# The recurrence stage of a one-core encoder step: two-operand work moved from GpSimd to VectorE, small products in the chunk banks, the elementwise stage cut in two

## The chip, the core and the metric

The kernel runs on one core of a Trainium2 chip. The metric is the device time of one execution in microseconds (us), less is better. A core has a matrix engine (TensorE, PE in the rows; PEld is its weight load), VectorE (DVE), ScalarE (ACT), GpSimd (POOL) and SyncE (SP). Each engine takes its instructions in the order in which they stand in its own queue, and waits on semaphores for the others. [...]

## The reference

One layer for two groups of requests at once, a prompt of 1024 tokens and 8 streams of 16 tokens: 1152 rows in all. The left branch of the layer is a recurrence over tokens:

```python
h = rms_norm(x, norm1_g)
p = h @ w_in                     # one projection: recurrence | attention | gates
u = pr + (shifted - pr) * mu     # token shift
r, k, v, wl, al, gl = split(u)
decay = exp(-exp(-softplus(-(w0 + tanh(wl) @ w2)) - 0.5))
a = sigmoid(a0 + al @ a2);  g = sigmoid(gl) @ g2
kk = k * k_k;  kk = kk * rsqrt(sum(kk * kk) + 1e-12)      # per head
k = k * (1 + (a - 1) * k_a)
# per token and head:
#   S = S * decay + (S @ -kk) (kk * a)^T + v k^T ;  y = S @ r
y = groupnorm(y) * lnx_g + lnx_b
o_a = (y + sum(r * k * r_k) * v) * g
o_b = forgetting_attention(...)
x = x + (sigmoid(g_a) * (o_a @ p_a) + sigmoid(g_b) * (o_b @ p_b)) @ w_out
x = x + swiglu(rms_norm(x))
```

There are 8 heads of 64, d_model is 1024, all in float32 (matrix products in two parts, high and low).

## The kernel before

The program runs through four stages. From 0 to 198 us x is normalised and turned, and the first tiles of the input projection are made. From 198 to 838 us the recurrence runs, from 838 to 1100 us the attention, and to the end the merge, the output product and the feed-forward part.

**The recurrence** goes by six units of 192 tokens (`rwkv_unit`, L527): five of the prompt, with 3 chunks of 64, and a last one whose second and third chunk's worth are the eight streams. A unit first writes the factors `BK` (L541 to L543) and `TT` (L550, L552), transposes v (L558), and makes the gram products (L587) in three rounds of four chunk-heads. Masks follow: `masked` (L572) on VectorE for the half that goes to `GB`, a copy by ScalarE (L590) and then a mask by GpSimd (the call behind L592) for the half that goes into `TT`. Then comes the inverse of a triangular factor: the copies L603, the half `goff` (L605, GpSimd), 15 steps of L616 and L618 on VectorE, transposes L630 and L632, and four groups of products of 32x32 (L651, L659 and L662, L679, L688), with the additions to `x1c` and `x3` by VectorE between (recorded at L387, the helper `hi`, which gives an instruction a high priority). Then the chunks, one after the other: the state product into `cp` (L724), the decayed state `sts` (GpSimd), `solve_u` (L707: VectorE copies `w_sb`, TensorE multiplies at L714, VectorE and ScalarE copy the two halves back), the product with the keys into `cp` (L736), the new state `st` by VectorE, and the outputs (L731, L747).

**Beside a unit** run two generators. `prologue` (L422) of the next unit makes its decays, norms and factors, with small products at L437/L438 and L446, exponentials, and the elementwise lines L484 to L491. `epilogue` (L500) of the unit before makes the group norm (L505, L511) and the gate product (L523). `step(nxt)` and `step(last)` run them on to their next `yield`; so the places of these calls in the unit set the order on TensorE.

**The projection** fills TensorE's gaps. It is a queue `fq` of 1032 pieces (43 weight tiles of 24 pieces; a piece is three products of 128x384, L151 to L153), from which `D(n)` takes n; `W(us)` (L389) takes as many as us / 0.52, rounded up. A weight tile is loaded by `load_w` (L139): a DMA, a rounded copy `hi_c` by ScalarE (L145), and the residue `lo_c` (L146), which `w_in_tile` (L211) gives to GpSimd. Pieces that are not taken by the end of the stage are taken at the attention.

**The order** on TensorE is the order of the code (a manual schedule). On the other engines a scheduler sets it before the program is built; each engine then works strictly in that order.

**PSUM** has eight banks: three of `gm` for the projection, two of `ms` for all small products, and one each of `y0`, `y1` (a unit's outputs) and `ch` (the chunk's `cp`).

In the rows, all buffers of the tag `t` are called t, whatever variable they hold.

Of the kernel before, what the change touches and what calls it, by code (L numbers as in the profile page):

```python
# [8 lines left out]
F32 = mybir.dt.float32  # L9
# [44 lines left out]
def hybrid_kernel(ctx: ExitStack, tc: tile.TileContext, d, o):  # L54
# [156 lines left out]
    def w_in_tile(c0, M):  # L211
        return load_w(wp1, d["w_in"][0, :, c0:c0 + M].rearrange("(k p) m -> p k m", p=P), NK, M, f"c{c0}", eng=GP)

# [140 lines left out]
    def ms():  # L354
        return psr.tile([P, 512], F32, tag="ms", name="ms")

    def tt_(tag="t", bufs=NSLOT):
        return rp.tile([P, W2], F32, tag=tag, name=tag, bufs=bufs)
# [15 lines left out]
    def pr4(t_):  # L374
        return t_.rearrange("p (y t) -> p y t", y=4)
# [46 lines left out]
    def prologue(u_, us, out):  # L422
# [10 lines left out]
        for z in range(2):  # L433
            pw, pa_ = ms(), ms()
            for y in (2 * z, 2 * z + 1):
                cs = slice((y % 2) * UT, (y % 2 + 1) * UT)
                T.matmul(pw[:, cs], lw[0:64, y * P:(y + 1) * P], LT[0:64, :], start=True, stop=True)  # L437
                T.matmul(pa_[:, cs], lw[64:128, y * P:(y + 1) * P], LT[64:128, :], start=True, stop=True)  # L438
            for y in (2 * z, 2 * z + 1):
                cs = slice((y % 2) * UT, (y % 2 + 1) * UT)  # L440
                S.activation(sw[:, y * UT:(y + 1) * UT], pw[:, cs], AF.Sigmoid, bias=pc("rwkv_w0", y))
                S.activation(a[:, y * UT:(y + 1) * UT], pa_[:, cs], AF.Sigmoid, bias=pc("rwkv_a0", y))
            yield
        for gs in HALF:
            ps = ms()
            T.matmul(ps[:, :2 * UT], ones_b, kk[:, gs], start=True, stop=True)  # L446
            S.activation(kk[:, gs], ps[:, :2 * UT], AF.Ln, bias=kkb)
# [27 lines left out]
        if ncp == NC3:  # L475
            V.tensor_tensor(sc[:, :, 0:ncp - 1], sc[:, :, 0:ncp - 1], dmn[:, :, 1:ncp], op=mult)
        else:
            scs = rp.tile([P, 4, NB], F32, tag="scs", name="scs", bufs=1)
            S.copy(scs.unsqueeze(3), pr4(dd)[:, :, C:UT].rearrange("p x (b t) -> p x b t", t=DT)[:, :, :, DT - 1:DT])

        k2 = tt_()
# [18 lines left out]
    def epilogue(u_, yT, bv, LG):  # L500

        sq = tt_()
        for gs in HALF:
            ps = ms()
            T.matmul(ps[:, :2 * UT], ones_b, yT[:, gs], start=True, stop=True)  # L505
            V.scalar_tensor_tensor(yT[:, gs], in0=ps[:, :2 * UT], scalar=-1.0 / C, in1=yT[:, gs], op0=mult, op1=add)
        S.activation(sq, yT, AF.Square)
        yield
        for gs in HALF:
            ps = ms()  # L510
            T.matmul(ps[:, :2 * UT], ones_b, sq[:, gs], start=True, stop=True)  # L511
            S.activation(sq[:, gs], ps[:, :2 * UT], AF.Ln, bias=gnb, scale=1.0 / C)
# [7 lines left out]
        for z, gs in enumerate(HALF):  # L520
            ps = ms()
            for y in range(2):
                T.matmul(ps[:, y * UT:(y + 1) * UT], lg[:, (2 * z + y) * P:(2 * z + y + 1) * P], LG, start=True, stop=True)  # L523
            V.tensor_tensor(yT[:, gs], yT[:, gs], ps[:, :2 * UT], op=mult)
        dma2(oa_s.rearrange("(c p) t -> p c t", p=P)[:, :, u_ * UT:(u_ + 1) * UT], pr4(yT))

    def rwkv_unit(u_, us, nu, pre, last):  # L527
# [14 lines left out]
        V.tensor_tensor(BK[:, :, 2, :], ch3(k2), ch3(e3), op=mult)  # L542
        GP.tensor_tensor(BK[HS[1], :, 0, :], ch3(k2)[HS[1]], ch3(e3)[HS[1]], op=mult)  # L543

# [6 lines left out]
        for hd in range(2):  # L551
            GP.tensor_tensor(TT[HS[hd], :, hd, 1, :], ch3(ur)[HS[hd]], ch3(e2)[HS[hd]], op=mult)  # L552
        SV = [ch3(tt_()) for _ in range(2)]
# [17 lines left out]

        def masked(dst, src, c0, hs, eng=V):  # L572
            n0 = 0
            late_ = [final and (c0 + n) % NC3 >= 1 for n in range(4)]
            while n0 < 4:
                n1 = n0 + 1
                while n1 < 4 and late_[n1] == late_[n0]:
                    n1 += 1
                mk = (gmask_s if late_[n0] else gmask)[hs].unsqueeze(1).broadcast_to([hs.stop - hs.start, n1 - n0, 2, C])
                eng.tensor_tensor(dst[:, n0:n1], src[hs, n0:n1], mk, op=mult)  # L580
                n0 = n1

        for c0 in range(0, NC12, 4):
            pg = [psr.tile([P, 4, 2, C], F32, tag="ms", name="gram") for _ in range(2)]
            for c in range(4):
                for hd in range(2):
                    T.matmul(pg[hd][:, c], both(hd, c0 + c), TT[HS[hd], c0 + c, hd], start=True, stop=True)  # L587
            for hd in range(2):
                masked(GB[HS[hd], c0:c0 + 4], pg[hd], c0, HS[hd])
                S.copy(TT[OP[hd], c0:c0 + 4, hd], pg[hd][OP[hd]])  # L590
            W(2.1)
        step(last)  # L592
        for hd in range(2):
            for c0 in range(0, NC12, 4):
                masked(TT[OP[hd], c0:c0 + 4, hd], TT[:, c0:c0 + 4, hd], c0, OP[hd], GP)
        gab, grb = GB[:, :, 0, :], GB[:, :, 1, :]
# [7 lines left out]
        goff = tt_()[:, 0:NC12 * 32].rearrange("p (c t) -> p c t", t=32)  # L604
        GP.tensor_tensor(goff, dg[:, 0:NC12, :], low16.unsqueeze(1).broadcast_to([P, NC12, 32]), op=mult)  # L605
        L = inv_tile()
# [25 lines left out]
        V.transpose(XL[:, 0:32, :], X[:, 0:32, :])  # L632
        step(nxt)
        step(last)
        W(2.6)
        step(nxt)
        W(2.1)
        step(nxt)
        W(2.1)
        step(nxt)  # L640
        step(last)
        W(4.2)
        xd = XL[:, 0:32, 0:NC12].rearrange("p t c -> p c t")
        QS = [slice(32 * q, 32 * q + 32) for q in range(4)]
        NB32 = NC12 * 32
        step(nxt)

# [6 lines left out]
        p03 = p0.rearrange("p (c t) -> p c t", t=32)  # L654
        W(1.0)
        ps, ps1 = ms(), ms()
# [45 lines left out]
        Y = [psr.tile([P, 2, NC3, C], F32, tag=f"y{z}", name=f"yps{z}", bufs=1) for z in range(2)]  # L702

# [3 lines left out]
        def solve_u(cp, c, y0, n):  # L707
# [8 lines left out]
            hi(S.copy, SV4[1][HS[1], ysl, c, :], cp[HS[1], 1, ysl])  # L716
            W(1.0)

        for c in range(ncp):
            cp = psr.tile([P, 2, 4, 64], F32, tag="ch", name="cp", bufs=1)  # L720
            for y in range(4):
# [4 lines left out]
            for hd, hs in enumerate(HS):  # L726
                hi(GP.tensor_tensor, sts[hs], SV4[hd][hs, :, c, :], sc[hs, :, c:c + 1].broadcast_to([64, 4, 64]), op=mult)
            for y in range(4):
# [31 lines left out]
        def streams(z):  # L760
# [16 lines left out]
            for cc in range(2):  # L777
                c = 1 + cc
                bsl = slice(4 * cc, 4 * cc + 4)
                bm = bds.unsqueeze(2).broadcast_to([P, 4, 64])  # L780
                cp = psr.tile([P, 2, 4, 64], F32, tag="ch", name="cps", bufs=1)
                ams = []
# [970 lines left out]
```

## Time and profile before

| | before |
|---|---|
| median of 3 runs | 2134.14 us (2127.28 to 2136.34) |
| the profiled execution | 2131.44 us |
| its span | 2129.7 us |
| TensorE busy, share of the span | 1987.0 us, 93% |
| VectorE | 1215.4 us, 57% |
| ScalarE | 835.1 us, 39% |
| GpSimd | 408.6 us, 19% |
| mean granted clock of TensorE | 0.966 |

TensorE is busy for 93% of the span. Its clock is granted between half and full speed by the chip, and a matmul in a stretch with a low clock counts as busy for longer. The table is a mean over stages with different limits; the rows below take the recurrence apart.

### The profile page before, as it was taken

The numbers are of one execution on the slowest core, as the hardware profiler recorded it, in microseconds if no ns is written. First come the engines' busy times: TensorE is split into PE (matmuls) and PEld (weight loads), VectorE is DVE, ScalarE is ACT, GpSimd is POOL, SyncE is SP. The second block draws the span as 40 slices with busy tenths as digits, with TensorE's granted clock in tenths as the row PEclk, the third lists the DMA queues.
The fourth block names the chain that finished last, engine by engine and source line by source line (L and its number), as shares of the span: only waits on it lengthen the run. The fifth ranks groups of instructions, "written<-read, shape, count | busy, mean of one in ns | idle before, by whom it ended". The sixth has DMA issues, their size and how long they took to land. (4 is left out here: it accounts for less than half of the span.)

```text
span 2129.7 us, 38310 instructions
## 1 busy us (share of the span) xinstructions
PE 1987.0 (93%) x15472; PEld 1803.2 (85%) x15472; DVE 1215.4 (57%) x2267; ACT 835.1 (39%) x1606; POOL 408.6 (19%) x445
## 2 busy tenths in 40 slices
PE   7999988889999998979989899999999999799998
PEld 7998877778787887767877799899999999788887
DVE  5112576555746645467755617966666666464445
ACT  5323444463635432456654325532332233121113
POOL 3322423233342410010015326000000000000004
PEclk9999999999999999889989999999999999899999
DMA  5332333222221223776547535232122221542212
GB/s 169 102 99 88 105 93 91 64 62 68 64 65 53 74 65 90 193 196 166 155 152 259 190 114 175 70 97 70 63 82 63 82 85 53 204 148 84 84 64 89
DMA packets 221541, 228.42 MB, mean 107 GB/s; under 512 B 41534, under 2 KB 195796, under 8 KB 221364
## 3 DMA queue, kind: packets, MB, share of 16 engines
q1 hardware_dynamic: 158916, 159.33, 25.3%
q10 hardware_dynamic: 61920, 64.54, 9.0%
q8 instruction: 122, 2.00, 0.4%
q0 software_dynamic: 528, 2.10, 0.3%
q14 instruction: 55, 0.45, 0.1%
HBM read 157.00 MB, written 68.98 MB: 106 GB/s over the span
## 5 line engine op out<-in xcount | busy, mean ns | idle before, releaser
L151 PE MATMUL gm<-hh,hi_c 128*128 128x384 f32 (+1 forms) x1032 | 376.3, 365 | 0.9 <-DVE vl L927 0.5
L153 PE MATMUL gm<-hh,lo_c 128*128 128x384 f32 (+1 forms) x1032 | 353.8, 343 | 1.6 <-POOL lo_c L146 1.6
L152 PE MATMUL gm<-hl,hi_c 128*128 128x384 f32 (+1 forms) x1032 | 354.6, 344 | 0.0
L151 PEld LDWEIGHTS gm<-hh,hi_c 128*128 128x128 f32 (+1 forms) x1032 | 198.0, 192 | 16.7 <-issue 3.1
L152 PEld LDWEIGHTS gm<-hl,hi_c 128*128 128x128 f32 (+1 forms) x1032 | 197.9, 192 | 4.7 <-issue 0.8
L153 PEld LDWEIGHTS gm<-hh,lo_c 128*128 128x128 f32 (+1 forms) x1032 | 197.5, 191 | 4.4 <-POOL lo_c L146 2.2
L1684 POOL TENSOR_TENSOR yo<-x,gF 128x512 f32<-128x512 f32 x17 | 21.9, 1289 | 760.8 <-DVE x L1668 751.1
L1664 PE MATMUL dn<-hi_d,ah 128*128 128x512 f32 x396 | 156.1, 394 | 12.4 <-ACT ah L1371 11.3
L1665 PE MATMUL dn<-lo_d,ah 128*128 128x512 f32 x396 | 155.4, 393 | 0.0
L1666 PE MATMUL dn<-hi_d,al 128*128 128x512 f32 x396 | 155.0, 393 | 0.0
L146 POOL TENSOR_TENSOR lo_c<-raw_c,hi_c 128x1024 fp32r<-128x1024 f32 (+1 forms) x43 | 103.3, 2403 | 245.6 <-ACT hi_c L145 243.2
L1668 DVE TENSOR_TENSOR x<-x,dn 128x512 f32<-128x512 f32 x108 | 73.9, 687 | 118.8 <-PE dn L1666 115.9
L1664 PEld LDWEIGHTS dn<-hi_d,ah 128*128 128x128 f32 x396 | 75.2, 190 | 29.3 <-ACT ah L1371 12.2
L265 DVE SCALAR_TENSOR_TENSOR su<-gm,omu,sh 128x384 f32<-128x384 f32 (+1 forms) x42 | 24.1, 573 | 122.5 <-ACT sh L261 95.9
L1666 PEld LDWEIGHTS dn<-hi_d,al 128*128 128x128 f32 x396 | 75.2, 190 | 16.3 <-DVE al L1372 0.5
L1665 PEld LDWEIGHTS dn<-lo_d,ah 128*128 128x128 f32 x396 | 75.3, 190 | 15.4
L1371 ACT CAST ah<-raw_act 128x1152 fp32r<-128x1152 f32 x22 | 25.6, 1162 | 159.7 <-PE dn L1665 141.4
L1469 PE MATMUL po<-hi_o,mh 128*128 128x256 f32 x288 | 82.5, 287 | 0.0
L1470 PE MATMUL po<-lo_o,mh 128*128 128x256 f32 x288 | 82.3, 286 | 0.0
L1471 PE MATMUL po<-hi_o,ml 128*128 128x256 f32 x288 | 82.1, 285 | 0.0
L145 ACT CAST hi_c<-raw_c 128x1024 fp32r<-128x1024 f32 (+1 forms) x43 | 44.3, 1031 | 74.1 <-PE gm L152 60.4
L1552 DVE TENSOR_TENSOR buf<-buf,m 128x256 f32<-128x256 f32 (+1 forms) x88 | 39.8, 453 | 45.4 <-PE m L1530 45.4
(495 smaller groups left out, 5482.2 us busy)
## 6 DMA issues: line engine op xcount, KB each, us to landing
raw_c<-in_w_in SPq DMA_DIRECT2D x42, 512.0 KB
raw_act<-a_s SPq DMA_DIRECT2D x22, 576.0 KB
raw_w_gate<-in_w_gate SPq DMA_DIRECT2D x22, 512.0 KB
raw_w_up<-in_w_up SPq DMA_DIRECT2D x22, 512.0 KB
raw_d<-in_w_down SPq DMA_DIRECT2D x22, 512.0 KB
g_s<-sg ACTq DMA_DIRECT2D x48, 192.0 KB
raw_o<-in_w_out SPq DMA_DIRECT2D x16, 512.0 KB
u_s<-su ACTq DMA_DIRECT2D x42, 192.0 KB
```

Of the source, the lines that this page charges most:

```text
L145: S.copy(hi[:, :, c0:c0 + M], raw)
L146: eng.tensor_tensor(lo[:, :, c0:c0 + M], raw, hi[:, :, c0:c0 + M].bitcast(F32), op=sub)
L151: T.matmul(ps, wh(k), xh(k), start=(k == 0), stop=False)
L152: T.matmul(ps, wh(k), xl(k), start=False, stop=False)
L153: r = T.matmul(ps, wl(k), xh(k), start=False, stop=(k == nk - 1))
L1469: T.matmul(ps[:, :Q], mh, hi, start=(k == 0), stop=False)
L1470: T.matmul(ps[:, :Q], mh, lo, start=False, stop=False)
L1471: T.matmul(ps[:, :Q], ml, hi, start=False, stop=(k == NK - 1))
L1664: T.matmul(ps, ah[:, ts_], wh[:, cs], start=(x == 0), stop=False)
L1665: T.matmul(ps, ah[:, ts_], wl[:, cs], start=False, stop=False)
L1666: T.matmul(ps, al[:, ts_], wh[:, cs], start=False, stop=(x == n - 1))
L1668: r = V.tensor_tensor(xs, xs, ps, op=add)
```

## The change

It does four things.

1. *GpSimd loses its work with two operands.* The residue `lo_c`, the third block of `BK`, the halves of `TT` with `ur * e2`, `goff` and `sts` go to VectorE. GpSimd keeps fills and copies.
2. *Masks from PSUM.* Both halves of the gram products are masked by VectorE straight from PSUM. ScalarE's copies (L590) and the masks of GpSimd are gone. The second round of grams uses the banks y0 and y1 in place of `ms`.
3. *Small products through the chunks' banks.* A new helper `xs` gives out y0, y1 and ch in turn; the products L437, L446, L505, L511 and L523 use it. The bonus product (L496) stays in `ms`.
4. *The elementwise stage in two parts.* `prologue` has one more `yield`, ahead of `k2`. What stands behind it (L484 to L491) is now run on by a `step(nxt)` behind the inverse's additions. The calls of `step` and `W` between the transposes of the inverse and its first product are placed anew, `W` behind `p0` and behind the additions takes more, and the last chunk's `W` too.

In the code after the change the lines have other numbers: L387 is L395, L437 is L445, L446 is L454, L484 is L493, L491 is L500, L505 is L514, L511 is L520, L523 is L532, L541 is L550, L550 is L559, L552 is L561, L580 is L589, L659 is L669, L714 is L726, L724 is L736 and L736 is L748.

```diff
     def w_in_tile(c0, M):
-        return load_w(..., NK, M, f"c{c0}", eng=GP)
+        return load_w(..., NK, M, f"c{c0}")
...
+    turn = [0]
+    def xs():
+        turn[0] += 1
+        tag = ("y0", "y1", "ch")[turn[0] % 3]
+        return psr.tile([P, 512], F32, tag=tag, name="xs", bufs=1)
...
-            pw, pa_ = ms(), ms()
+            pw, pa_ = xs(), xs()
...
-            ps = ms()
+            ps = xs()
             T.matmul(ps[:, :2 * UT], ones_b, kk[:, gs], start=True, stop=True)
...
+        yield
         k2 = tt_()
...
-        GP.tensor_tensor(BK[HS[1], :, 0, :], ch3(k2)[HS[1]], ch3(e3)[HS[1]], op=mult)
+        V.tensor_tensor(BK[HS[1], :, 0, :], ch3(k2)[HS[1]], ch3(e3)[HS[1]], op=mult)
...
-            GP.tensor_tensor(TT[HS[hd], :, hd, 1, :], ch3(ur)[HS[hd]], ch3(e2)[HS[hd]], op=mult)
+            V.tensor_tensor(TT[HS[hd], :, hd, 1, :], ch3(ur)[HS[hd]], ch3(e2)[HS[hd]], op=mult)
...
-            pg = [psr.tile([P, 4, 2, C], F32, tag="ms", name="gram") for _ in range(2)]
+            pg = [(psr.tile([P, 512], F32, tag=f"y{x}", name="gram", bufs=1) if c0 == 4 else ms())
+                  .rearrange("p (c y t) -> p c y t", c=4, y=2) for x in range(2)]
...
                 masked(GB[HS[hd], c0:c0 + 4], pg[hd], c0, HS[hd])
-                S.copy(TT[OP[hd], c0:c0 + 4, hd], pg[hd][OP[hd]])
+                masked(TT[OP[hd], c0:c0 + 4, hd], pg[hd], c0, OP[hd])
             W(2.1)
         step(last)
-        for hd in range(2):
-            for c0 in range(0, NC12, 4):
-                masked(TT[OP[hd], c0:c0 + 4, hd], TT[:, c0:c0 + 4, hd], c0, OP[hd], GP)
...
-        GP.tensor_tensor(goff, dg[:, 0:NC12, :], low16..., op=mult)
+        V.tensor_tensor(goff, dg[:, 0:NC12, :], low16..., op=mult)
...
         step(nxt)
+        W(1.5)
         step(last)
-        W(2.6)
+        W(1.5)
         step(nxt)
-        W(2.1)
+        W(1.5)
         step(nxt)
-        W(2.1)
+        W(1.5)
+        step(last)
+        W(1.0)
         step(nxt)
-        step(last)
-        W(4.2)
+        W(1.5)
+        step(nxt)
+        W(3.1)
...
-        step(nxt)
...
         hi(S.copy, p0, ps[:, :NB32])
-        W(1.0)
+        W(2.1)
...
                 hi(GP.memset, x3[qs, :, 0:32], 0.0)
-        W(2.1)
+        step(nxt)
+        W(2.6)
...
-            W(1.0)
+            W(1.5 if c == ncp - 1 else 1.0)
...
-                hi(GP.tensor_tensor, sts[hs], ...)
+                hi(V.tensor_tensor, sts[hs], ...)
...
         for _ in prologue(0, us, pre):
-            W(6.0)
+            W(5.0)
```

In all 636 pieces of the projection stand in the recurrence stage, 621 before; 330 stand ahead of it (332 before), and 66 are left for behind it (79 before).

Three places of the new order follow, all in the third unit that makes a next one (unit 2 by the code's count). On TensorE, ahead of the inverse's first product, stand the norm product of the next unit (line 446; `ones_b` is a constant of block sums) and the gate product of the unit before (line 523), among pieces of the projection (lines 151 to 153). Before:

```order
L153 MATMUL gm<-hh_100,lo_c_5285 128x384
L151 MATMUL gm<-hh_100,hi_c_5284 128x384
L152 MATMUL gm<-hl_103,hi_c_5284 128x384
L153 MATMUL gm<-hh_100,lo_c_5285 128x384
L446 MATMUL ms<-t,ones_b 128x384 x2
L523 MATMUL ms<-lo_3309,lg 128x192 x4
```

After, where the norm product is line 454 and the gate product line 532:

```order
L532 MATMUL xs<-lo_3312,lg 128x192 x4
L151 MATMUL gm<-hh_98,hi_c_5399 128x384
L152 MATMUL gm<-hl_101,hi_c_5399 128x384
L153 MATMUL gm<-hh_98,lo_c_5400 128x384
L151 MATMUL gm<-hh_98,hi_c_5399 128x384
L152 MATMUL gm<-hl_101,hi_c_5399 128x384
L153 MATMUL gm<-hh_98,lo_c_5400 128x384
L454 MATMUL xs<-t,ones_b 128x384 x2
```

The gate product has moved ahead of the norm product, with two pieces between, and both take a bank from `xs`.

On VectorE, from the elementwise stage of the next unit to the first chunk (`w_sb` is the copy that the chunk's second product reads; the rows of 32 partitions are the additions to `x1c` and `x3`). Before:

```order
L485 TENSOR_TENSOR u<-t,u 128x768
L487 TENSOR_TENSOR t<-t 128x768
L491 SCALAR_TENSOR_TENSOR t<-u,prm 128x192 x4
L541 SCALAR_TENSOR_TENSOR BK<-t 128x12x64
L542 TENSOR_TENSOR BK<-u,t 128x12x64
L387 TENSOR_TENSOR t<-ms,inv 32x384 x2
L387 TENSOR_TENSOR t<-ms,inv 32x12x32 x4
L387 COPY w_sb<-cp 128x256
L387 COPY t<-cp 64x4x64
```

After:

```order
L146 TENSOR_TENSOR lo_c_4820<-raw_c_4817,hi_c_4819 128x1024
L395 TENSOR_TENSOR t<-ms,inv 32x384 x2
L395 TENSOR_TENSOR t<-ms,inv 32x12x32 x4
L493 TENSOR_SCALAR t<-t,prm,oka 128x192 x4
L494 TENSOR_TENSOR u<-t,u 128x768
L496 TENSOR_TENSOR t<-t 128x768
L500 SCALAR_TENSOR_TENSOR t<-u,prm 128x192 x4
L550 SCALAR_TENSOR_TENSOR BK<-t 128x12x64
L551 TENSOR_TENSOR BK<-u,t 128x12x64
L395 COPY w_sb<-cp 128x256
L552 TENSOR_TENSOR BK<-u,t 64x12x64
L395 COPY t<-cp 64x4x64
```

The additions have moved ahead of the second part (lines 493 to 500) and of two blocks of the next unit's `BK`; `w_sb` now stands behind all of these, and a residue (line 146) ahead of the additions. In the other units with a next one the order is alike; the residue stands right ahead of the additions in four units of the six.

On VectorE, the last chunk of the same unit, with the new state `st` at its end. Before:

```order
L387 COPY w_sb<-cp 128x256
L550 TENSOR_TENSOR TT<-t 64x12x64 x2
L387 COPY t<-cp 64x4x64
L387 TENSOR_TENSOR st<-cp,sc 128x256
L387 TENSOR_TENSOR st<-st,sts 128x256
```

After:

```order
L395 COPY w_sb<-cp 128x256
L559 TENSOR_TENSOR TT<-t 64x12x64 x2
L395 COPY t<-cp 64x4x64
L146 TENSOR_TENSOR lo_c_5202<-raw_c_5199,hi_c_5201 128x1024
L561 TENSOR_TENSOR TT<-u,t 64x12x64
L395 TENSOR_TENSOR st<-cp,sc 128x256
L561 TENSOR_TENSOR TT<-u,t 64x12x64
L395 TENSOR_TENSOR st<-st,sts 128x256
```

Behind the copy of `cp` into t a residue and the first half of `ur * e2` (line 561) have come ahead of the state, and the second half stands between its two instructions.

## Rows read from the trace of the kernel before

**Rows 1.** busy time by stage: start:end, us, each engine's busy time (count), granted clock, DMA
```profile
198.00:838.00 640.00, 579.63 (x6347) 501.71 (x6346) 376.73 (x678) 293.59 (x532) 203.77 (x175) 0.95 0.25 74
838.00:861.00 23.00, 18.29 (x98) 17.38 (x96) 10.26 (x17) 2.87 (x7) 3.21 (x3) 0.85 0.62 155
```

**Rows 2.** waits of TensorE, 198 to 838 us: line, releaser, total us, times, longest
```profile
PE ms L523 <- ACT t L447: 14.0, 4, 6.8
PE cp L736 <- ACT t L387: 10.9, 5, 3.5
PE ms L511 <- ACT t L627: 7.9, 3, 4.4
PE ms L437 <- ACT t L441: 6.3, 4, 2.2
PE lfps L859 <- DVE sg L853: 4.9, 1, 4.9
PE ms L659 <- ACT t L387: 4.1, 2, 3.7
```

**Rows 3.** timeline, unit 3: start us, us, engine, line, operation, idle before
```profile
476.22 1.05 ACT L447 ACTIVATE t<-ms,kkb 128x384 f32<-128x384 f32 x2
476.85 2.93 PE L523 MATMUL ms<-lo,lg 128*128 128x192 f32 x8 [6.82 <-ACT t L447]
```

**Rows 4.** timeline, VectorE and GpSimd side by side
```profile
357.06 2.42 POOL L146 TENSOR_TENSOR lo_c<-raw_c,hi_c 128x1024 fp32r<-128x1024 f32 x1 [6.21 <-ACT hi_c L145]
357.30 2.32 DVE L616 TENSOR_TENSOR tmp<-inv 128x128 f32<-128x128 f32 x1
361.18 0.86 ACT L627 COPY t<-ms 128x384 f32<-128x384 f32 x2 [3.38 <-DVE inv L618]
```

**Rows 5.** timeline, last chunk of a unit
```profile
513.43 3.46 DVE L550 TENSOR_TENSOR TT<-t 64x768 f32<-64x768 f32 x2
513.48 5.09 POOL L552 TENSOR_TENSOR TT<-u,t 64x768 f32<-64x768 f32 x2 [0.93 <-PE yps L731]
516.92 0.42 DVE L387 COPY t<-cp 64x256 f32<-64x256 f32 x1
517.84 0.69 PE L736 MATMUL cp<-t 128*64 128x64 f32 x16 [1.86 <-ACT t L387]
```

**Rows 6.** timeline, unit 5 from the additions to the first chunk
```profile
671.26 5.16 DVE L387 TENSOR_TENSOR t<-ms,inv 32x384 f32<-32x384 f32 x6 [1.35 <-PE ms L662]
678.20 0.43 DVE L387 COPY w_sb<-cp 128x256 f32<-128x256 f32 x1 [1.77 <-PE cp L724]
679.28 0.68 PE L714 MATMUL cp<-w_sb,t 64*64 64x64 f32 x16
```

**Rows 7.** timeline, elementwise stage of unit 2
```profile
386.54 1.25 DVE L484 TENSOR_SCALAR t<-t,prm,oka 128x192 f32<-128x192 f32 x4
387.82 0.96 DVE L485 TENSOR_TENSOR u<-t,u 128x768 f32<-128x768 f32 x1
```

**Rows 8.** the instructions of line 491: ns min/median/max, first and last start
```profile
L491 DVE SCALAR_TENSOR_TENSOR t<-u,prm x24: 405/408/2537, 216.4 to 667.8; 128x192 f32<-128x192 f32 x24
```

**Rows 9.** busy time in windows of 4 us, columns as in rows 1
```profile
224.00:228.00 4.00, 1.97 (x8) 1.98 (x9) 3.99 (x7) 0.00 (x0) 0.00 (x0) 0.63 0.79 226
228.00:232.00 4.00, 4.00 (x15) 4.00 (x14) 2.29 (x7) 1.81 (x3) 0.00 (x0) 0.52 0.53 157
```

**Rows 10.** groups of GpSimd, 198 to 838 us: busy us, mean ns, idle before, releasers
```profile
L146 POOL TENSOR_TENSOR lo_c<-raw_c,hi_c 128x1024 fp32r<-128x1024 f32 x26 | 63.1, 2428 | 122.5 <-ACT hi_c L145 120.1 <-issue 1.9 <-POOL sts L387 0.3
L580 POOL TENSOR_TENSOR TT<-TT,gmask 64x512 f32<-64x512 f32 (+1 forms) x38 | 42.0, 1106 | 35.4 <-ACT TT L590 33.9
L552 POOL TENSOR_TENSOR TT<-u,t 64x768 f32<-64x768 f32 x12 | 30.1, 2508 | 11.9 <-ACT t L469 8.2 <-PE yps L731 3.3
L387 POOL TENSOR_TENSOR sts<-t,sc 64x256 f32<-64x256 f32 x32 | 22.0, 689 | 77.5 <-DVE t L387 76.5
```

**Rows 11.** groups of VectorE, whole program
```profile
L1372 DVE TENSOR_TENSOR lo_d<-raw_d,hi_d 128x1024 fp32r<-128x1024 f32 x22 | 26.8, 1221 | 10.7 <-ACT hi_d L1371 10.7
```

More of the change, by code (lines that the diff above doesn't have):

```diff
@@ L211, in w_in_tile @@
     def w_in_tile(c0, M):
-        return load_w(wp1, d["w_in"][0, :, c0:c0 + M].rearrange("(k p) m -> p k m", p=P), NK, M, f"c{c0}", eng=GP)
+        return load_w(wp1, d["w_in"][0, :, c0:c0 + M].rearrange("(k p) m -> p k m", p=P), NK, M, f"c{c0}")
     ahead = []
@@ L503, in epilogue @@
         for gs in HALF:
-            ps = ms()
+            ps = xs()
             T.matmul(ps[:, :2 * UT], ones_b, yT[:, gs], start=True, stop=True)
@@ L509, in epilogue @@
         for gs in HALF:
-            ps = ms()
+            ps = xs()
             T.matmul(ps[:, :2 * UT], ones_b, sq[:, gs], start=True, stop=True)
@@ L520, in epilogue @@
         for z, gs in enumerate(HALF):
-            ps = ms()
+            ps = xs()
             for y in range(2):
@@ L570, in rwkv_unit, with masked @@
         GB = rp.tile([P, NC12, 2, C], F32, tag="GB", name="GB", bufs=1)
-        def masked(dst, src, c0, hs, eng=V):
+        def masked(dst, src, c0, hs):
             n0 = 0
@@ L579, in masked @@
                 mk = (gmask_s if late_[n0] else gmask)[hs].unsqueeze(1).broadcast_to([hs.stop - hs.start, n1 - n0, 2, C])
-                eng.tensor_tensor(dst[:, n0:n1], src[hs, n0:n1], mk, op=mult)
+                V.tensor_tensor(dst[:, n0:n1], src[hs, n0:n1], mk, op=mult)
                 n0 = n1
         for c0 in range(0, NC12, 4):
-            pg = [psr.tile([P, 4, 2, C], F32, tag="ms", name="gram") for _ in range(2)]
+            pg = [(psr.tile([P, 512], F32, tag=f"y{x}", name="gram", bufs=1) if c0 == 4 else ms())
+                  .rearrange("p (c y t) -> p c y t", c=4, y=2) for x in range(2)]
             for c in range(4):
@@ L604, in rwkv_unit @@
         goff = tt_()[:, 0:NC12 * 32].rearrange("p (c t) -> p c t", t=32)
-        GP.tensor_tensor(goff, dg[:, 0:NC12, :], low16.unsqueeze(1).broadcast_to([P, NC12, 32]), op=mult)
+        V.tensor_tensor(goff, dg[:, 0:NC12, :], low16.unsqueeze(1).broadcast_to([P, NC12, 32]), op=mult)
         L = inv_tile()
@@ L701, in rwkv_unit @@
                 hi(V.tensor_tensor, SV4[hd][hs, :, 0, :], st[hs], dmn[hs, :, 0:1].broadcast_to([64, 4, 64]), op=mult)
-        Y = [psr.tile([P, 2, NC3, C], F32, tag=f"y{z}", name=f"yps{z}", bufs=1) for z in range(2)]
+        Y = [psr.tile([P, 512], F32, tag=f"y{z}", name=f"yps{z}", bufs=1)[:, 0:2 * UT]
+             .rearrange("p (y c t) -> p y c t", y=2, c=NC3) for z in range(2)]
         def yout(z):
@@ L716, in solve_u @@
             hi(S.copy, SV4[1][HS[1], ysl, c, :], cp[HS[1], 1, ysl])
-            W(1.0)
+            W(1.5 if c == ncp - 1 else 1.0)
         for c in range(ncp):
-            cp = psr.tile([P, 2, 4, 64], F32, tag="ch", name="cp", bufs=1)
+            cp = psr.tile([P, 512], F32, tag="ch", name="cp", bufs=1).rearrange("p (z y t) -> p z y t", z=2, y=4)
             for y in range(4):
@@ L726, in rwkv_unit @@
             for hd, hs in enumerate(HS):
-                hi(GP.tensor_tensor, sts[hs], SV4[hd][hs, :, c, :], sc[hs, :, c:c + 1].broadcast_to([64, 4, 64]), op=mult)
+                hi(V.tensor_tensor, sts[hs], SV4[hd][hs, :, c, :], sc[hs, :, c:c + 1].broadcast_to([64, 4, 64]), op=mult)
             for y in range(4):
@@ L780, in streams @@
                 bm = bds.unsqueeze(2).broadcast_to([P, 4, 64])
-                cp = psr.tile([P, 2, 4, 64], F32, tag="ch", name="cps", bufs=1)
+                cp = psr.tile([P, 512], F32, tag="ch", name="cps", bufs=1).rearrange("p (z y t) -> p z y t", z=2, y=4)
                 ams = []
```

## The prediction

> **What bounds the kernel now.** I read the busy time by stage first. In the recurrence stage, 198 to 838 us, TensorE works 579.63 us of 640, VectorE 376.73, ScalarE 293.59 and GpSimd 203.77, and the granted clock is 0.95 [rows 1]. TensorE is therefore the bound, but with two holes: the time in which it stands, about 60 us, and the clock, (1 - 0.95) x 640 = 32 us of full-speed work. No other engine is full, so what an edit is worth is what it does to the waits of TensorE.
>
> So I went next to the waits of TensorE in that stage [rows 2]. Six of them hold 48.1 us in 19 waits. Line 523 (the gate product of the epilogue) waits 14.0 us, four times; line 736 (the state product) 10.9, five times; line 511 (the variance product) 7.9; line 437 (the decay products of the prologue) 6.3; line 859 (a transpose of the projection) 4.9; line 659 (the inverse's second product) 4.1.
>
> Then I looked in the timeline at what each of them really waits for. Line 523 waits 6.82 us in unit 3 and starts as soon as ScalarE has read the first half of the norm product (line 447, at 476.22 us) [rows 3]. The gate product needs nothing of line 447. It needs a buffer of the two that `ms` has, and both hold norm products. Line 511 is of the same kind: it waits for ScalarE's copy L627, the reader of the key transposes, which is not its input either [rows 2]. Behind that there is a second cause: GpSimd's L146 runs from 357.06 to 359.48 us, and VectorE's L616, 128 short elements a partition, starts 0.24 us later and ends at 359.62, just after it; ScalarE's copy stands 3.38 us behind VectorE's chain [rows 4]. Line 736 has the same pair behind it: two instructions L550 of VectorE take 3.46 us beside two L552 of GpSimd (5.09 us), the next copy of VectorE starts only at 516.92, and TensorE stands 1.86 us [rows 5].
>
> These rows read as a lock: a VectorE instruction with two operands in SBUF does not go on while GpSimd has one in hand. The Trainium skill says the same ("SBUF — State Buffer", section "SBUF: two separate sides"): the port pair that the two engines share is given to one of them for a whole instruction and the other blocks fully. The trace agrees (2.32 us for L616); by that rule the change would get VectorE's time back, not TensorE's, and the sum below needs only the rows.
>
> **The change part by part.**
> *Two-operand work leaves GpSimd.* In the stage GpSimd has 26 L146 of 2428 ns, 48 masks (38 in the row shown), 12 L552 and 32 `sts` [rows 10], beside six L543 and six L605. On VectorE an L146 should take what the same subtraction takes later in the program, 1221 ns [rows 11]: 26 x 1.22 = 32 us more load, the rest some 30 us more, and about 40 us of lock time back. So VectorE stands near 377 + 62 - 40 = 400 of 640 us and does not become the bound by its sum. What matters is where those instructions stand in its order.
>
> *Last chunk.* L550 no longer meets L552, so two of L550 cost about 1.9 us in place of 3.46 and one more piece lies ahead of line 736. The five waits of 10.9 us [rows 2] fall to about 1.6: -9.3. Now L146 and the halves of `ur*e2` stand near the state's instructions there; that is priced below.
>
> *Products in the idle banks.* The gate product now comes ahead of the norm product and takes a bank of y0, y1 and ch. Its cause is gone: -14.0. Line 511 has a bank of its own: -7.9. Line 859 waits for VectorE's L853 once, behind a locked chain: -4.9. All three from [rows 2]. The decay products rotate over three banks where two pairs need four, so the second pair still waits for the first's reader; cover falls from 5 pieces to 3. I keep its 6.3 us (bounds 0 and 11.5). Line 659 is not touched: 4.1 stays (0 to 8.2).
>
> *The elementwise stage in two parts.* This is the step that costs. The second part is put behind the inverse's additions, and in VectorE's new order it stands ahead of the first chunk's `w_sb`, for which the first chunk's second product waits. Its length: line 484 1.25 us, four instructions of 128x768 at 0.96 (lines 485, 487, 541, 542) [rows 7], four of line 491 at 0.405, its minimum [rows 8]: 1.25 + 3.84 + 1.62 = 6.7 us. In unit 5 of before, the additions start at 671.26, `w_sb` at 678.20 and the product that reads it at 679.28, 8.0 us after the additions; VectorE is idle for 1.77 us before `w_sb` [rows 6]. After: additions about 5.1, part two 6.7, `w_sb` 0.4: ready at 12.2 us, where TensorE wants it at 8.0. The number of pieces between does not change. So TensorE gets a new wait of about 4 us, in units 0 to 4 (the last has no next unit): +20. Bounds: 2.4 us each if TensorE runs at a low clock there and comes later, 5.2 if L146 falls between: 12 to 26; below that only if the order on the chip hides it (rival B).
>
> *L146 and the halves on VectorE ahead of chain work.* In four units an L146 stands right ahead of the additions, in some ahead of the state. I take 4 x 1.2 plus a little: +6 (0 to 12).
>
> *Clock.* Each wait costs more than itself: from 224 to 228 us TensorE works 1.97 of 4 us and the granted clock is 0.63 of full speed (2.4 GHz); in the next 4 us, where it works all the time, it is 0.52, the lower level of 1.2 GHz for nearly all of it [rows 9]. 32 us over 19 waits is 1.7 us each. Thirteen waits go (4 + 3 + 1 + 5), five come: 8 x 1.7 = 14 us back (0 to 32).
>
> The Trainium skill says of this ("TensorE: Matmul & The Clock Gate", section "HAM oscillation — how this bites in real kernels") that repeated gaps of TensorE throw its clock back each time. By that rule gaps that are only moved give no clock back, the term of 14 us would be 0 and the time near 2121. That is rival C, priced below from rows.
>
> *Pieces.* Thirteen pieces of the projection move from behind the stage into it (0.52 us each, 6.8 us). They are work either way, and in the stage they fill waits that I have already counted: 0 (-7 to +7). Behind the stage the short stretch of 838 to 861 us has TensorE busy 18.29 of 23 us at a clock of 0.85 [rows 1], so little is lost or won there.
>
> **Sum.** -14.0 - 7.9 - 4.9 - 9.3 + 20 + 6 - 14 = -24. The profiled execution took 2131.4 us (span 2129.7), 2.7 below the median of 2134.1. 2131.4 - 24 = 2107, and from the median 2110. I give **2108**.
>
> **The rivals.**
> *A, slower: VectorE stands behind the residues.* L146 needs ScalarE's L145 first, and GpSimd waited for that 120.1 us in 26 times, 4.6 each [rows 10]. On GpSimd nothing is behind it. On VectorE, which works in order, everything is: the inverse's chain, the copies of the chunks. If half of the 26 stand so for half of that wait, 13 x (2.3 + 1.2) = 45 us more, 2107 + 45 = 2152. It decides from 38 us on, where 2107 passes 2145, 1.5 us for each of the 26. Against it: GpSimd's wait counts from its own last instruction, often long before, and VectorE has 240 us of room.
> *B, the second part is hidden.* If the additions end earlier (their 5.16 us in unit 5 hold a lock with an L146 [rows 6]) or more work of TensorE lies ahead, the new wait is gone with its clock: 2107 - 20 - 5 x 1.7 = 2079. Against it: the order puts all of part two ahead of `w_sb`.
> *C, the clock does not come back.* The waits that are left and the five new ones keep it at 0.95: 2107 + 14 = 2121, with the upper bound of the new wait 2127: at the edge of 0.5% and within it. For it speaks that the new waits are long (4 us).
> *D, the masks and residues were off the path and nothing of their removal shows:* only the waits of the ring and of line 859 go (-26.8), the new ones come (+20): 2131.4 - 6.8 = 2125, within 0.5% too. Against it stand rows 4 and 5, in which the lock reaches TensorE.
>
> **How the numbers follow.** Forecast (2093 to 2122) 0.42; B 0.20; C and D 0.23; A 0.15. 0.5% is about what a measurement of this kernel tells from no change, 10.7 us: below 2123.5 is faster, above 2144.8 slower. Faster: 0.40 of the forecast and 0.20 of B, 0.60. Same: 0.02, 0.23 and a fifth of A (its weak end), 0.28. Slower: 0.12. The range goes from B, 2077, to the point where A begins to count, 2140.
>
> **What would show it.** Right: no wait at the gate product and the variance product; L491's successor at a mean near 405 ns, not 1067; a new wait of TensorE for `w_sb`, about 4 us, five times; the state product's wait below 0.5 us; a stage shorter by 20 to 30 us at a clock of 0.96 or more. Wrong: a stage as long as before with TensorE waiting for VectorE's residues or copies behind an L146 (A), or no `w_sb` wait at all (B), or the same clock with fewer waits (C). The prediction falls altogether if the first part of the elementwise stage, which now runs beside other VectorE work, makes the inverse late.

## The result and the profile after

The changed kernel takes 2107.86 us, the median of 4 runs (2106.34 to 2110.43), where the kernel before took 2133.06 us, the median of four; in the jobs of the experiments below it took 2127 to 2129. The ratio is 0.9899, with a 95% interval of 0.988 to 0.9918: 1% faster. The profiled execution has a span of 2108.4 us against 2129.7. The forecast was 2108. One execution of a later kernel took 2714.26 us at a granted clock of 0.649, far from its others, and is left out of that kernel's time.

First the busy time by stage again, cut where the attention's first product starts (line 991 before, 1003 after): each engine's busy time (count), then the granted clock. Before:

```profile
198.00:839.08 641.08, 580.71 (x6354) 502.70 (x6353) 377.42 (x679) 293.62 (x532) 203.77 (x175) 0.95 0.25 74
```

After:

```profile
198.00:826.07 628.07, 584.86 (x6432) 508.99 (x6432) 422.68 (x810) 269.32 (x497) 22.95 (x47) 0.96 0.27 78
```

Two things are to be seen here. In the stage TensorE stands 641.08 - 580.71 = 60.4 us before and 628.07 - 584.86 = 43.2 us after: 17 us fewer. And it works 4.2 us longer there although it makes 25 more pieces of the projection in that window (648 products of line 151 against 623), which is 13 us of work: the other work, and the same work, therefore cost some 9 us less, and the granted clock is 0.96 instead of 0.95. The stage ends 13.0 us earlier. Behind it the program (2129.7 - 839.1 = 1290.6 us before, 2108.4 - 826.1 = 1282.3 after) is 8.3 us shorter, since by this cut 20 pieces fewer are left for it (10.4 us of work; the other 5 were made ahead of 198 us in the kernel before). VectorE has gone from 377 to 423 us, GpSimd from 204 to 23.

Then the waits of TensorE in the stage after, which answer to [rows 2] (line, releaser, total, times, longest):

```profile
PE ms L699 <- ACT t L395: 19.8, 10, 4.4
PE xs L446 <- ACT t L449: 4.6, 5, 1.6
PE xs L446 <- ACT t L521: 4.4, 1, 4.4
PE ms L669 <- ACT t L395: 1.4, 2, 1.2
PE cp L748 <- ACT t L395: 0.3, 1, 0.3
```

The gate product and the variance product (lines 523 and 511 before, 532 and 520 after) are not in the list any more, nor is the forget gate's transpose, line 859 before. The product with the keys (line 748, 736 before), which the prediction calls the state product, has 0.3 us left of 10.9. A new wait has come, at line 699, the last small product of the inverse: 19.8 us, ten times.

The group of the residues on VectorE (count, busy, mean ns, then idle time ahead), and the successor of the instruction in [rows 8] (min/median/max in ns):

```profile
L146 DVE TENSOR_TENSOR lo_c<-raw_c,hi_c 128x1024 fp32r<-128x1024 f32 x27 | 33.0, 1221 | 27.8 <-ACT hi_c L145 27.7
```

```profile
L500 DVE SCALAR_TENSOR_TENSOR t<-u,prm x24: 405/411/414, 219.7 to 663.3; 128x192 f32<-128x192 f32 x24
```

The residue takes 1.2 us as estimated from [rows 11], and line 500 no longer has one long instance: its largest is 414 ns, before 2537.

Last, the place in which the new wait arises, from the timeline of the changed kernel (start, duration, engine, idle time ahead and what ended it):

```profile
475.78 1.23 DVE L146 TENSOR_TENSOR lo_c<-raw_c,hi_c 128x1024 fp32r<-128x1024 f32 x1 [2.57 <-ACT hi_c L145]
476.93 5.06 DVE L395 TENSOR_TENSOR t<-ms,inv 32x384 f32<-32x384 f32 x6
482.02 2.07 DVE L493 TENSOR_SCALAR t<-t,prm,oka 128x192 f32<-128x192 f32 x4
484.12 0.96 DVE L494 TENSOR_TENSOR u<-t,u 128x768 f32<-128x768 f32 x1
485.17 0.97 ACT L395 COPY t<-ms 32x384 f32<-32x384 f32 x2 [6.02 <-DVE u L494]
485.69 0.31 PE L699 MATMUL ms<-t 32*32 32x32 f32 x2 [4.20 <-ACT t L395]
489.04 0.42 DVE L395 COPY w_sb<-cp 128x256 f32<-128x256 f32 x1
```

VectorE ends the additions at 482.0 us and goes on to the second part of the elementwise stage. ScalarE's copy (`p1`, for which the product at line 699 waits) starts only when VectorE's line 494 has ended, at 485.1. TensorE stands 4.20 us. VectorE's `w_sb` comes at 489.04, and TensorE's wait for it is 0.3 us in the whole stage.

### The profile page after: what moved, and what is told of

The parts are those of the page before. It is cut to its first block, busy times and chain, and to the rows that moved or that the text cites. A ratio compares the mean times of both kernels' runs of the same rounds, so it can differ in the third digit from the quotient of the medians.

```text
span 2108.4 us, 38216 instructions
## 1 busy us (share of the span) xinstructions
PE 1980.6 (94%) x15472; PEld 1796.7 (85%) x15472; DVE 1276.6 (61%) x2414; ACT 808.4 (38%) x1567; POOL 187.1 (9%) x298
## 5 line engine op out<-in xcount | busy, mean ns | idle before, releaser
L146 DVE TENSOR_TENSOR lo_c<-raw_c,hi_c 128x1024 fp32r<-128x1024 f32 (+1 forms) x43 | 51.5, 1199 | 70.2 <-ACT hi_c L145 70.1
```

Of the source, the lines that this page charges most:

```text
L146: eng.tensor_tensor(lo[:, :, c0:c0 + M], raw, hi[:, :, c0:c0 + M].bitcast(F32), op=sub)
```

## The experiments

Ratios are to the kernel before, run in the same job (its median there was 2127 to 2129 us; against 2127 the change itself would stand at 0.991), with 95% intervals.

**p1 without a slot of its own.** The scheduler lays `p1` in a slot of the tag t. Is it that slot that waits, or is the second part too long for VectorE?

```diff
-        p0 = tt_()[:, 0:NB32]
+        p01 = tt_()
+        p0 = p01[:, 0:NB32]
...
-        p1 = tt_()[:, 0:NC12 * 32]
+        p1 = p01[:, NB32:2 * NB32]
```

> The changed kernel, with one edit: the small copy p1 of the inverse (384 columns) takes the unused upper half of the tile of p0 in place of a new slot of the tag t. Nothing is left out of the computation. Theory S (slot): the ten waits of line 699 in the changed kernel (19.8 us) are ScalarE's copy p1 waiting for a slot whose last reader is VectorE's line 494 in the second part of the elementwise stage; with another place for p1 they go, and since the scheduler now sets w_sb ahead of line 500, TensorE's wait there is at most 1.5 us in five units: 2085 to 2095 us. Rival D (work): the second part of the elementwise stage is simply too long for VectorE ahead of the first chunk, and the same 4 us a unit come back at w_sb (line 726): 2103 to 2112 us, with 15 to 20 us of waits at line 726.

Measured: 2089.64 us, ratio 0.982 (0.9795 to 0.9844). The waits of TensorE at the two places, and the same stretch of the timeline:

```profile
PE cp L727 <- DVE w_sb L395: 8.5, 6, 1.9
```

```profile
471.05 5.03 DVE L395 TENSOR_TENSOR t<-ms,inv 32x384 f32<-32x384 f32 x6
475.26 0.97 ACT L395 COPY t<-ms 32x384 f32<-32x384 f32 x2 [0.40 <-PE ms L691]
480.08 0.42 DVE L395 COPY w_sb<-cp 128x256 f32<-128x256 f32 x1
480.65 0.77 PE L727 MATMUL cp<-w_sb,t 64*64 64x64 f32 x16 [0.96 <-DVE w_sb L395]
```

The copy now waits 0.40 us, for the product that it reads, and starts at 475.26, four microseconds into the additions. The waits of the inverse's last product are gone. What is left stands at `w_sb` (line 727 here): 8.5 us in six waits, 1.4 each and 1.9 at most, where 1.5 or less in five was expected. So the slot was the cause of the waits at line 699. The 18 us of time by the medians are not the slot's alone: the order on VectorE changed with it, as the scheduler now sets `w_sb` ahead of lines 500 and 550.

**The second part ahead of the inverse's first product.**

```diff
-        step(nxt)          # behind the additions
         W(2.6)
...
+        step(nxt)          # ahead of the inverse's first product
         ps = ms()
```

> The changed kernel, with the step that runs the second part of the elementwise stage moved back: ahead of the inverse's first product (line 661) in place of behind the additions. Nothing is left out. Both S and D expect the waits at line 699 to go, as p1's slot is then free early. S and D: VectorE does the second part while TensorE makes pieces and two groups of products, the additions wait at most 1 us a unit for it: 2083 to 2095 us. Rival E (the place behind the additions is right): the additions now stand behind 6.7 us of VectorE work, and lines 690 or 669 wait for them 3 to 5 us a unit: 2103 to 2115 us.

Measured: 2085.33 us, ratio 0.9797 (0.9777 to 0.9817). The waits at line 699 are gone but for 1.7 us, and the additions are not late:

```profile
PE ms L670 <- ACT t L395: 7.0, 4, 3.3
PE ms L699 <- DVE t L395: 1.7, 3, 0.6
```

```profile
459.37 0.84 ACT L477 ACTIVATE t<-t 128x768 f32<-128x768 f32 x1
460.12 0.46 ACT L395 COPY t<-ms 128x384 f32<-128x384 f32 x1
460.63 1.54 PE L670 MATMUL ms<-inv,t 32*32 32x32 f32 x96 [1.17 <-ACT t L395]
466.52 1.14 PE L690 MATMUL ms<-t,GB 32*32 32x32 f32 x48 [0.23 <-DVE t L395]
```

7.0 us stand at line 670 now. The timeline shows what they wait for: ScalarE's copy `p0` starts when its exponential of line 477 has gone through, at 460.12 us; TensorE follows at 460.63.

**The same with one piece fewer ahead of the inverse's first product and two more behind p0's copy.** By the rounding of `W` the first number takes 5 pieces in place of 6, the second 7 in place of 5.

```diff
         step(nxt)
-        W(3.1)
+        W(2.1)
...
         hi(S.copy, p0, ps[:, :NB32])
-        W(2.1)
+        W(3.6)
```

> The changed kernel with the second part of the elementwise stage ahead of the inverse's first product (as in the run with that edit alone, 2085 us, ratio 0.980) and two pieces moved from ahead of that product to behind p0's copy, where TensorE still waited 7.0 us for ScalarE's p0. Nothing is left out. Expected: those 7.0 us fall to 2 to 4, ratio 0.976 to 0.980. Rival: with less work ahead of it the inverse's transposes come late, and line 661 waits instead: 0.980 to 0.983.

> The same kernel as the last of the runs before (second part ahead of the inverse's first product, two more pieces behind p0's copy), for its profile, which was taken in a disturbed execution. Expected: ratio 0.976 to 0.980 again; waits at line 669's place 2 to 4 us in all against 7.0; no wait at w_sb or p1 over 1 us.

Measured: 2077.92 us and, the same kernel again, 2078.37 us, ratios 0.9778 (0.9736 to 0.982) and 0.9758 (0.9737 to 0.9779). Waits of TensorE in the stage, the second time; line 670, where 2 to 4 us were expected, is not in the list:

```profile
PE xs L446 <- ACT t L449: 8.5, 5, 3.2
PE xs L446 <- ACT t L521: 3.1, 1, 3.1
```

What is left first is line 446, the second pair of decay products in the rotation of three banks, 11.6 us in six waits. This kernel is 2.2 to 2.4% faster than the kernel before. Against the changed kernel with the second part ahead alone (0.9777 to 0.9817) its medians are 7 us lower, but the intervals meet, so a gain in time by this last edit is not shown; that the waits at line 670 went is shown.

**Only the residues on VectorE, in the kernel before.**

```diff
-        return load_w(..., NK, M, f"c{c0}", eng=GP)
+        return load_w(..., NK, M, f"c{c0}")
```

> The kernel before, with one part of the change alone: the residues of line 146 go to VectorE, the other GpSimd work stays. Nothing is left out. Theory L (lock): the wait of 4.9 us at line 859 goes and part of the waits of line 511 (7.9), with 1.7 us of clock for each of up to four waits: 2133 - 5 - 3 - 4 = 2119 to 2127 us. Rival A (VectorE stands behind the residues, as in the prediction): new waits of TensorE on chains of VectorE behind a residue, 2138 to 2155 us. Rival N (residues were off the path): 2130 to 2136 us.

Measured: 2113.14 us, ratio 0.9923 (0.9901 to 0.9946). 14 us below the kernel before in the same job, at the upper end of theory L (6 to 14 below), and the opposite of rival A. The steps of the inverse on VectorE (line 616, ns min/median/max), before and here:

```profile
L616 DVE TENSOR_TENSOR tmp<-inv x90: 191/263/2355, 264.9 to 732.2; 128x30 f32<-128x30 f32 x12, 128x56 f32<-128x56 f32 x12, 128x78 f32<-128x78 f32 x12, 128x96 f32<-128x96 f32 x12
```

```profile
L616 DVE TENSOR_TENSOR tmp<-inv x90: 181/259/293, 264.8 to 718.4; 128x30 f32<-128x30 f32 x12, 128x56 f32<-128x56 f32 x12, 128x78 f32<-128x78 f32 x12, 128x96 f32<-128x96 f32 x12
```

The longest of the 90 instructions falls from 2355 to 293 ns. Waits of TensorE, and the stage as a window:

```profile
PE ms L523 <- ACT t L447: 12.5, 3, 6.3
PE cp L736 <- ACT t L387: 8.5, 5, 1.9
PE lfps L859 <- DVE sg L853: 3.2, 1, 3.2
PE ms L511 <- ACT t L627: 2.3, 3, 1.1
PE ms L659 <- ACT t L387: 2.3, 2, 1.9
```

```profile
198.00:825.69 627.69, 575.59 (x6362) 495.69 (x6361) 385.71 (x706) 292.74 (x533) 140.89 (x151) 0.96 0.26 76
```

Each row of [rows 2] is smaller, line 511 by 5.6 us, line 736 by 2.4, lines 859 and 659 by 1.7 and 1.8. One wait for VectorE is longer, line 151 behind VectorE's line 927 (3.5 us, 0.5 before), the largest trace of rival A. TensorE stands 627.69 - 575.59 = 52.1 us in place of 60.4, and it works 575.59 us in place of 580.71 although three more pieces lie in the window. VectorE is busy for 385.71 us, 8.3 more than before, though it took over 26 residues of 1.2 us, 32 us in all: so some 24 us of stretched instructions are gone. By the ratios one line of the change gives about three quarters of its gain (0.77 of 1.01%); the two were measured in different jobs and their intervals meet, so the share is rough.

**Only the residues back on GpSimd, in the changed kernel.**

```diff
-        return load_w(..., NK, M, f"c{c0}")
+        return load_w(..., NK, M, f"c{c0}", eng=GP)
```

> The changed kernel with one part undone: the residues of line 146 go back to GpSimd, all else stays. Nothing is left out. Theory L: the lock beside an L146 is what the change mainly took away, so instructions of VectorE with two operands in SBUF take 2 us and more again beside it and TensorE's waits grow by 6 to 13 us: ratio to the kernel before 0.994 to 0.999 (the change: 0.990). Rival W: with the masks and the other GpSimd work gone and the products in another order, an L146 on GpSimd costs nothing more, and VectorE has 32 us less to do: ratio 0.985 to 0.991.

Measured: 2118.30 us, ratio 0.9961 (0.9941 to 0.9981). Theory L has the time: 0.6% come back. The steps of the inverse (line 616 is line 623 here; in the change its longest takes 293 ns), the waits and the stage:

```profile
L623 DVE TENSOR_TENSOR tmp<-inv x90: 190/259/2325, 259.3 to 727.3; 128x30 f32<-128x30 f32 x12, 128x56 f32<-128x56 f32 x12, 128x78 f32<-128x78 f32 x12, 128x96 f32<-128x96 f32 x12
```

```profile
PE ms L699 <- ACT t L395: 12.7, 10, 2.9
PE xs L446 <- ACT t L449: 6.6, 5, 2.1
PE ms L632 <- ACT t L634: 4.0, 1, 4.0
```

```profile
198.00:832.30 634.30, 589.48 (x6405) 511.61 (x6404) 408.70 (x781) 268.91 (x495) 86.12 (x71) 0.95 0.26 76
```

The long instructions beside an L146 are back, but not as the waits of 6 to 13 us that theory L had: line 699 waits less than in the change (12.7 against 19.8), lines 446 and 632 a few microseconds more, and in sum TensorE stands 634.30 - 589.48 = 44.8 us, 1.6 more than in the change. The larger part is in its work: 589.48 us against 584.86, with some seven pieces (3.6 us) fewer, at a granted clock of 0.95 against 0.96.

**Only the rest back on GpSimd.** The third block of `BK`, the halves of `TT`, `goff` and `sts`:

```diff
-        V.tensor_tensor(BK[HS[1], :, 0, :], ...)
+        GP.tensor_tensor(BK[HS[1], :, 0, :], ...)
...
-            V.tensor_tensor(TT[HS[hd], :, hd, 1, :], ...)
+            GP.tensor_tensor(TT[HS[hd], :, hd, 1, :], ...)
...
-        V.tensor_tensor(goff, ...)
+        GP.tensor_tensor(goff, ...)
...
-                hi(V.tensor_tensor, sts[hs], ...)
+                hi(GP.tensor_tensor, sts[hs], ...)
```

> The changed kernel with the other half of its first part undone: the third block of BK, the halves ur*e2 of TT, goff and the decayed state sts go back to GpSimd; the residues stay on VectorE and the masks stay as changed. Nothing is left out. Theory B (both halves count): the state product waits again beside L561 on GpSimd, about 1.9 us five times, and sts and goff lock VectorE's chain copies: ratio to the kernel before 0.992 to 0.998. Rival F (first half alone counts): the residues were the whole of the lock's price, and these pieces of work go back at no cost: ratio 0.986 to 0.991.

Measured: 2121.20 us, ratio 0.9966 (0.9955 to 0.9978). Theory B. The product with the keys (line 748) waits again, `w_sb` too, and in the timeline the pair stands side by side once more:

```profile
PE cp L748 <- ACT t L395: 6.7, 5, 1.4
PE cp L726 <- DVE w_sb L395: 2.5, 4, 1.1
```

```profile
198.00:836.95 638.95, 590.88 (x6429) 513.37 (x6429) 408.13 (x754) 269.77 (x497) 94.04 (x103) 0.95 0.26 76
```

```profile
491.52 2.30 POOL L552 TENSOR_TENSOR BK<-u,t 64x768 f32<-64x768 f32 x1 [14.26 <-DVE u L494]
492.07 2.95 DVE L500 SCALAR_TENSOR_TENSOR t<-u,prm 128x192 f32<-128x192 f32 x4
```

Four instructions of line 500 that take 4 x 0.41 us alone take 2.95 us beside one L552 of GpSimd. In the stage TensorE stands 638.95 - 590.88 = 48.1 us, 4.9 more than in the change, and works 6.0 us longer with one piece fewer.

**Only the order of the two products, in the kernel before.**

```diff
-        step(nxt)
-        step(last)
-        W(4.2)
+        step(last)
+        W(1.0)
+        step(nxt)
+        W(3.6)
```

> The kernel before with one edit: the gate product of the epilogue (line 523) ahead of the norm product (line 446), two pieces of the projection between them, seven behind; the buffers of ms stay, GpSimd's work stays. Nothing is left out. Theory O (order): the 14.0 us of line 523 go and little takes their place: ratio to the kernel before 0.991 to 0.995. Rival R (banks): with two buffers the norm product or the next small product now waits as long for the gate product's reader on VectorE: ratio 0.997 to 1.002.

Measured: 2128.19 us, ratio 1.0005 (0.9983 to 1.0027): nothing. The waits, and ScalarE ahead of the inverse's second product (line 660 here):

```profile
PE ms L660 <- ACT t L387: 13.0, 6, 3.7
PE ms L446 <- DVE t L524: 2.5, 3, 2.0
```

```profile
484.67 0.85 ACT L448 ACTIVATE t<-t 128x768 f32<-128x768 f32 x1
485.42 0.83 ACT L465 ACTIVATE t<-t 128x768 f32<-128x768 f32 x1
486.89 0.82 ACT L469 ACTIVATE t<-t 128x768 f32<-128x768 f32 x1
487.86 0.47 ACT L387 COPY t<-ms 128x384 f32<-128x384 f32 x1
488.38 1.54 PE L660 MATMUL ms<-inv,t 32*32 32x32 f32 x96 [2.30 <-ACT t L387]
```

The 14.0 us of the gate product are gone, and line 660 has gone from 4.1 to 13.0 us. Rival R gave the time, but not for its reason: the norm product waits only 2.5 us for the gate product's reader. With the norm product later, ScalarE's four exponentials (lines 448, 465, 469 above and line 467 between) now stand ahead of the copy `p0` in its queue, and TensorE has two pieces of cover there. The waits moved.

**Both, in the kernel before.** The two edits above together (residues on VectorE, order of the products):

> The kernel before with two edits alone: the residues of line 146 on VectorE, and the gate product ahead of the norm product. Nothing is left out. If lock and order are separate causes (L and O both right), their gains add: 0.992 of the residues alone and 0.991 to 0.995 of the order give a ratio of 0.983 to 0.988, below the whole change (0.990). Rival P (shared): the two take away the same wait, and together they give no more than the residues alone: ratio 0.990 to 0.994.

Measured: 2115.67 us, ratio 0.9954 (0.9934 to 0.9973): the gains don't add. It is no more than the residues alone gave, as rival P has it, though its middle lies above rival P's 0.990 to 0.994; its interval meets that of the residues alone (0.9901 to 0.9946, in another job). Again the wait is at p0's copy:

```profile
PE ms L660 <- ACT t L387: 11.9, 5, 3.1
```

**The rotation of the banks undone, in the changed kernel.**

```diff
     def xs():
-        turn[0] += 1
-        tag = ("y0", "y1", "ch")[turn[0] % 3]
-        return psr.tile([P, 512], F32, tag=tag, name="xs", bufs=1)
+        return ms()
```

> The changed kernel, with the helper that rotates the three chunk banks giving out the two buffers of ms again: the order of the code stays as in the change. Nothing is left out. Theory R (ring): the waits at the variance product and the gate product come back, 14 + 8 us at most and less as the gate product now stands ahead of the norm product, with their clock: 2118 to 2135 us. Rival O (order): it was the order of the two products, not the banks, that took the waits away: 2105 to 2112 us.

Measured: 2112.85 us, ratio 0.993 (0.9904 to 0.9956), just outside rival O's time and below theory R's. Both were reckoned from the change's 2108 us, and by the ratios this run lies 7 us above the change, between the two, so the time does not decide. Its interval meets that of the change (0.988 to 0.9918): the banks are worth 5 us by the medians, 7 by the ratios, no more than the uncertainty, and not 22. The waits decide. Those at the places concerned:

```profile
PE ms L697 <- ACT t L393: 19.8, 10, 4.4
PE ms L443 <- ACT t L447: 6.1, 5, 2.1
PE ms L443 <- ACT t L519: 4.9, 1, 4.9
PE ms L452 <- DVE t L531: 3.8, 5, 1.2
```

The gate product and the variance product are not in the list with two buffers either; the decay and norm products wait 14.8 us here, in place of about 10 in the change.

## Why the prediction was right, and where not

The time was right to 0.2 us, and that closeness is chance: the four runs of the changed kernel lie 4 us apart, the median of the kernel before moved from 2133 to 2127 us between jobs, and the terms missed in both directions. Of the prediction's own signs four came: no wait at the gate and the variance product, line 500 at a mean of 411 ns, 0.3 us at line 748, a clock of 0.96. Two did not: the stage is 13 us shorter and not 20 to 30, and there is no new wait at `w_sb`.

*The locks* were read rightly, and were worth more than they were given. The prediction took 9.3 us at line 736 and 4.9 at line 859 from them, and nothing else by name. The run with the residues alone on VectorE gives 0.8% for one line, the two runs that undo one half each give 0.6 to 0.7% back. The Trainium skill ("SBUF — State Buffer", section "SBUF: two separate sides") names the pair of engines and the exclusive hold; the maximum of line 616, 2355 ns with and 293 ns without an L146 on GpSimd, agrees. VectorE's load came to 423 us and not near 400: what it took over besides the residues (masks, halves, `sts`, `goff`) is about 60 us by the rows of the change, where the prediction had 30. It did not become the bound by that.

*The ring.* The terms -14.0 for line 523 and -7.9 for line 511 failed in their reason. The waits are gone in the changed kernel, as the trace shows. But the banks are not why: with two buffers again neither product waits. And the gate product's 14 us cannot be had by taking its cause away: with the order changed alone its wait goes, the wait at p0's copy grows by 9 us, and the time stays (1.0005). "Its cause is gone" is not enough; the prediction should have said what is late next, and that is ScalarE's copy behind four exponentials. In the change the cover behind `p0` is five pieces instead of two, and line 669 waits 1.4 us. That the cover is what keeps the gain is read from this and from the kernel with seven pieces there, where 7.0 us went; no run gives the kernel before the new order and the longer cover. And 5.6 of the 7.9 us at line 511 were lock, not ring.

*The new wait* was right in size, wrong in place and in its last step. The prediction said 4 us in five units at `w_sb`, from the second part standing ahead of it on VectorE. Measured: 19.8 us in ten waits, two for each of five units, at line 699, the inverse's last product, because ScalarE's copy into a new slot had to wait for a reader in the second part. Both edits that free the slot early (another place for `p1`; the second part ahead) take these waits for ScalarE's copy away. VectorE's own sum was right: in the unit shown `w_sb` is ready at 489.04 + 0.42 - 476.93 = 12.5 us after the additions start, where the prediction had 12.2. TensorE had by then already stood at line 699. Whether 4 us would have stood at `w_sb` without the slot, in this order, no run shows: in the kernel with another place for `p1` the scheduler sets `w_sb` ahead of the longer half, and the wait there is 1.4 us. That the sum came out at 20 is partly chance.

*The clock* gave less than 14 us. By the stage's window, (1 - 0.96) x 628 = 25 us against 32 before: 7 us. The trace's clock records, averaged over the stage to three digits (0.947 and 0.962), give 34 and 24 us: 10. That the stage's work became some 9 us cheaper agrees. The waits gave more than the -10 us that the prediction had for them in sum: -17. The +6 for residues and halves ahead of chain work is the term that does not show: no wait of TensorE in the list stands behind them by name. The two misses nearly cancel. The two waits that were kept, 6.3 us at the decay products and 4.1 at line 659, came out at 9.0 and 1.4, the same in sum.

*Pieces* at 0: 25 more cost 13.0 us in the stage and the rest of the program is 8.3 us shorter, 4.7 us in sum, within the bounds. So 17 + 9 - 5 = 21 us, which is the difference of the two profiled spans.

*Rival A* falls by the run that is made for it: the residues on VectorE make the kernel faster, not slower. In the changed kernel's timeline VectorE waits 2.57 us for ScalarE's `hi_c` and starts the residue at 475.78 us, and the additions start 1.15 us after that; in this unit the residue delays them by its own length at most, which is what the term of +6 stood for. *Rival B* (2079 us, second part hidden) comes near the two faster kernels: at 0.980 and 0.976 they have the change without its stall. *Rivals C and D* don't describe the result: a part of the clock came back, and the residues' removal shows.

What stays open. How the gain of each half of the lock divides into waits and clock is seen in one profiled execution of each kernel: the residues alone take 8.3 us of standing away and make the work 7 us cheaper; undone, they bring 1.6 and 8 us; the other half, undone, 4.9 and 6.5. Executions of the kernel before differ by up to 19 us among themselves (2117 to 2136 us, with clocks of 0.975 to 0.964), so this division is rough. That TensorE's clock is lower because of the waits is argued from the two going together; no run changes one without the other. No run makes the masks straight from PSUM, where TensorE leaves the gram products, or the cut of the elementwise stage by itself; what either is worth is not shown.

## What to carry to other kernels

A wait that goes at one product is a gain only if the next one on the same chain has cover: look for the queue that is late next (here ScalarE's copies behind exponentials) and put the filler work there. A buffer that rotates through a shared ring ties its first writer to the last reader of whatever had the slot; before a step is moved on one engine, look which small copies on other engines take slots that it frees. Where VectorE has room (here 377 of 641 us busy), work with two operands on GpSimd can be worth moving even if GpSimd is idle for most of the time, as it was here.

## What the runs showed of the hardware

The price of the lock is not in GpSimd's own busy time. 26 residues, 63 us of a GpSimd that is idle for two thirds of the stage, cost 0.6 to 0.8% of the program. VectorE's instructions with two operands in SBUF, the core's working memory, are stretched beside them: the longest of line 616 takes 2355 ns before, 293 ns with the residues moved, and 2325 ns with them back on GpSimd in the changed kernel, at a median of 259 to 263 ns in all three. Over the stage that is some 24 us of VectorE's time. TensorE gains in two ways from their move: it stands 8.3 us less, and it needs 575.59 us, with three more pieces, for what took 580.71, at a granted clock of 0.96 in place of 0.95.
